# A transformer kernel with another order in its opening, and differential attention with the queries on the partitions

## The chip, the core and the metric

The kernel runs on one core of a Trainium2 chip. The metric is the device time of one execution in microseconds (us), lower is better. The engines have one instruction queue each and run what stands in it in that order: TensorE (PE in the profile; its weight loads are the row PEld), VectorE (DVE), ScalarE (ACT), GpSimd (POOL) and SyncE (SP, which only issues DMAs here; ACT issues some as well).

## The reference, cut to what matters

Two blocks for 512 tokens of width 1024, all float32. What the change touches:

```
# block 1, opening
mod = silu(c) @ w_ada + b_ada;  shift, scale, gate = split(mod, 3)
h = rms_norm(x, g_pre) * (1 + scale) + shift
proj = h @ w_in                      # forget gates, k and v of the window attention, ...
# block 2
mem_h = rms_norm(mem, mem_norm_g);   k, v = split(mem_h @ w_mem_kv, 2)   # 256 memory rows
k = rms_norm(k of 4 heads of 256)
# differential attention, 8 heads, two maps of depth 64 each, values 128 wide
p = softmax(q_m @ k_m.T * scale + bias, causal)       # m = 0, 1
a = p[0] - lam * p[1]
o = rms_norm(a @ v, subln_g) * (1 - lambda_init)
o = o * silu(gate);   y_diff = o @ w_proj
```

The rest (forgetting attention, window attention with sinks, convolution, cross attention to the memory, merging gates, projections) is computed by both kernels in the same way.

## The kernel before, in words

Every product of 1024-wide operands is made in three passes: an operand is split into a rounded part (`wh`, `hh`) and the rest (`wl`, `hl`), and hh·wh, hh·wl and hl·wh are summed in one PSUM bank. `load_w` fetches a weight chunk in four (512 columns) or two DMAs, ACT casts it to `wh` (L170), DVE or POOL subtracts to get `wl` (L172). `mm_T` (L202), `mm_N` (L213) and `mm_W` (L221) issue the matmuls. PSUM has eight banks: three `mm`, two `sc` (scores), two `tp` (transposes), one `pv`.

**Opening.** Everything in it is issued through `Ordered` (all its rows have L342), so that each engine keeps the written order. The memory rows `mt` are transposed to `mT`; `mem_k(0, ...)` makes the first half of the memory keys, 16 float32 matmuls of 512 columns, each of which the profile shows as two passes; `mem_k(1, ...)` makes the second half in four pieces that stand between the other work. x (`xn`) is squared, normalised and transposed (`x_transpose`) to `xt`. For each of the eight 128-wide slices k, 1 MB of `w_ada` (`ada`) is multiplied with silu(c): `products` does it on ACT and DVE with two matmuls at the end (`sums`), `sums_pe` does it wholly on PE, with 16 matmuls of one column. `modulate` and `hidden` then make `hh` and `hl` of that slice: ACT writes `hh`, DVE the exact value `ht`, POOL or DVE the difference. The first projection (`w1c`, 264 columns, 96 matmuls of L213) stands behind the opening, then `qb` (96 matmuls of 512 columns, L221). SP issues the DMAs of the opening in the written order. The scheduler of the language orders the rest by priorities and a model of its own.

**Middle.** Between the output projection of block 1 and block 2, `mem_v(0)` and `mem_v(1)` make the memory values, 48 matmuls each in three passes (`sc<-wh,mh` and so on, L221), while the two norms of the block end are computed.

**Differential attention.** `staged` runs over 32 pairs (head h, 128 queries n): `diff_sc` makes the scores of two maps and exponentials, `diff_tp` transposes the probabilities, `diff_pv` multiplies with the values. After each step `fill` issues a few matmuls of projections (`glu`, `dqk`, `dv`, gates) between them. DVE also does the convolution there, 248 instructions of 512 columns (`cv`, L1020) at the lowest priority. `diff_pv` works once per head, with values as weights: 12 matmuls of 512 to 128 columns give the output with the value index on the partitions. The norm over that index is then a sum over partitions: `rsum` (four one-column float32 matmuls), `rsqrt_small`, `rdiag` (four diagonal tiles on DVE, L260) and `rbc` (four float32 matmuls, L266).

Of the kernel before, what the change touches and what calls it, by code (L numbers as in the profile page):

```python
# [20 lines left out]
P = 128  # L21
# [71 lines left out]
def two_block_kernel(ctx: ExitStack, tc: tile.TileContext, A: dict, out: bass.AP):  # L93
# [137 lines left out]
    def rsqrt_small(wk, ss, n, inv, eps, tag, bufs=None):  # L231
# [4 lines left out]
        dve.tensor_scalar(out=v, in0=ss, scalar1=inv, scalar2=eps, op0=ALU.mult, op1=ALU.add)  # L236
# [106 lines left out]


    mT_d = dram.tile([P, KT, 256], F32, name="mT_d")
    mrs = const.tile([P, 2], F32, name="mrs")
    with ExitStack() as st:
# [3 lines left out]
        mt = pa.tile([P, 2, 1024], F32, tag="ada", name="mt", bufs=4)  # L351
# [3 lines left out]
        mk = pa0.tile([P, 2, 1024], F32, name="mk")  # L355
        kss = pa0.tile([P, 2, 4], F32, name="kss")
# [45 lines left out]
        pms = {}  # L402

        def sums(k):
            pms[k] = tp_tile()
            for j in range(2):
                pe.matmul(out=pms[k][:, j:j + 1], lhsT=accs[k][0][:, j * P:(j + 1) * P], rhs=ones[:, 0:1], start=True, stop=True)

        def sums_pe(k):
            pms[k] = tp_tile()  # L410
            for j in range(2):
                for i in range(KT):
                    pe.matmul(out=pms[k][:, j:j + 1], lhsT=adas[k][:, i, j * P:(j + 1) * P], rhs=cs[:, i:i + 1], start=(i == 0), stop=(i == KT - 1))

        def modulate(k):
            dve.scalar_tensor_tensor(out=mod[:, 2 * k:2 * k + 2], in0=pms[k][:, 0:2], scalar=0.5, in1=V("b_ada")[:, 2 * k:2 * k + 2], op0=ALU.mult, op1=ALU.add)
            dve.scalar_tensor_tensor(out=gs[:, k:k + 1], in0=mod[:, 2 * k + 1:2 * k + 2], scalar=1.0, in1=V("g_pre", k), op0=ALU.add, op1=ALU.mult)

        def hidden(k, eng):
            t = pa.tile([P, S], F32, tag="ht", name="ht", bufs=2)  # L420
            act.activation(out=hh[:, k, :], in_=xt[:, k, :], func=AF.Identity, scale=gs[:, k:k + 1], bias=mod[:, 2 * k:2 * k + 1])
            dve.tensor_scalar(out=t, in0=xt[:, k, :], scalar1=gs[:, k:k + 1], scalar2=mod[:, 2 * k:2 * k + 1], op0=ALU.mult, op1=ALU.add)
            eng.tensor_tensor(out=hl[:, k, :], in0=t, in1=f(hh[:, k, :]), op=ALU.subtract)

        kb_ = [None, None]

        def mem_k(c, ks_):
            if ks_[0] == 0:
                kb_[c] = [sc_tile() for t in range(2)]
            for k in ks_:  # L430
                for t in range(2):
                    pe.matmul(out=kb_[c][t], lhsT=mT[:, k, t * P:(t + 1) * P], rhs=raws[c][k // 2][:, k % 2, :], start=(k == 0), stop=(k == KT - 1))

        def mem_k_out(c):
            for t in range(2):
                act.activation(out=mk[:, t, c * NW:(c + 1) * NW], in_=kb_[c][t], func=AF.Copy, scale=mrs[:, t:t + 1])
# [22 lines left out]
        mem_k(0, range(KT))  # L459
# [3 lines left out]
        act.dma_start(out=mT_d, in_=mT)  # L463
        products(0, act)
        products(0, dve)
        products(1, act)
        products(1, dve)
        load_ada(4)
        dve.tensor_copy(out=mrs, in_=rsqrt_small(pa, mss, 2, 1.0 / 1024, 1e-6, "rn2"))
        squares(xn, xss, range(NT))  # L470
        mem_k_out(0)
        mem_k(1, range(2))
        sums(0)
        sums(1)
        r = rsqrt_small(pa, xss, NT, 1.0 / 1024, 1e-6, "rn4")
        for t in range(NT):
            dve.tensor_scalar(out=xn[:, t, :], in0=xn[:, t, :], scalar1=r[:, t:t + 1], scalar2=None, op0=ALU.mult)
        modulate(0)
        modulate(1)
        products(2, act)  # L480
        products(2, dve)
        load_ada(5)
        x_transpose(range(4))
        products(3, act)
        products(3, dve)
        raw_chunk(1, range(2, 4))
        load_ada(6)
        x_transpose(range(4, KT))
        mem_k(1, range(2, 4))
        sums(2)  # L490
        hidden(0, pool)
        hidden(1, pool)
        products(4, act)
        products(4, dve)
        load_ada(7)
        sums(3)
        modulate(2)
        sums_pe(5)
        hidden(2, pool)
        modulate(3)  # L500
        hidden(3, pool)
        sums(4)
        products(6, act)
        products(6, dve)
        modulate(4)
        hidden(4, pool)
        modulate(5)
        hidden(5, pool)
        mem_k(1, range(4, 7))
        sums(6)  # L510
        mem_k(1, range(7, 8))
        mem_k_out(1)
        sums_pe(7)
        modulate(6)
        hidden(6, dve)
        modulate(7)
        hidden(7, dve)
# [22 lines left out]
        with low(-ROTP):  # L540
# [4 lines left out]
            dve.tensor_scalar(out=sub8, in0=V("subln"), scalar1=0.8, scalar2=None, op0=ALU.mult)  # L545
# [7 lines left out]


        with low(LOWMK):
            for t in range(2):
                sq = xn[:, t, :]
                act.activation(out=sq, in_=mk[:, t, :], func=AF.Square)
                dve.tensor_reduce(out=kss[:, t, :], in_=sq.rearrange("p (h d) -> p h d", d=256), axis=AX.X, op=ALU.add)
            kr = rsqrt_small(pa0, kss.rearrange("p t h -> p (t h)"), 8, 1.0 / 256, 1e-6, "kr")  # L560
            for t in range(2):
                for h in range(4):
                    s = mk[:, t, h * 256:(h + 1) * 256]
                    dve.tensor_scalar(out=s, in0=s, scalar1=kr[:, t * 4 + h:t * 4 + h + 1], scalar2=None, op0=ALU.mult)
                nc.scalar.dma_start(out=k_d[:, t, :], in_=mk[:, t, :])
# [59 lines left out]
    with ExitStack() as stS:  # L625
# [18 lines left out]
        w = load_w(A["w1c"], 264)  # L644
        for t in range(NT):
            ps = mm_tile()
            mm_N(ps[:, 0:264], w, hh, hl, t, n=264)
            act.copy(out=natk[:, t, :], in_=ps[:, 0:256])
            dve.tensor_tensor(out=fz[:, t, :], in0=ps[:, 256:264], in1=V("fgate"), op=ALU.add)
# [256 lines left out]
    def mem_v(c, bank):  # L906
        if c == 0:
# [5 lines left out]
        mh, ml = MV[0]  # L913
        w = load_w(A["w_mem"][2 + c], NW)
        banks = [bank() for t in range(2)]
        yield from mm_W(banks, w, mh, ml, range(2))
        mv = mvp.tile([P, 2, NW], F32, tag="mv", name="mv")
        for t in range(2):
            act.activation(out=mv[:, t, :], in_=banks[t], func=AF.Copy, scale=mrs[:, t:t + 1])
        nc.scalar.dma_start(out=v_d[:, :, c * NW:(c + 1) * NW], in_=mv)  # L920
        yield

    with ExitStack() as st:
# [21 lines left out]
        for hf in range(2):  # L945
# [31 lines left out]
            run(mem_v(hf, sc_tile))  # L977
# [9 lines left out]
    with ExitStack() as st:  # L987
        wk = open_pool(st, "wk2", 2, reuse_waits="tile")
        dp = open_pool(st, "dp", 2, reuse_waits="tile")
        cm_[0] = open_pool(st, "cm2", 1, reuse_waits="tile")  # L990
# [152 lines left out]
        def diff_tp(it):  # L1143
            h, n = it
            causal_tp(it, D.pop(it), n, (n + 1) * P, ("dpt", h))
# [417 lines left out]
```

## Time and profile before

| | |
|---|---|
| median of 3 runs | 1201.15 us (1197.31 to 1202.04) |
| profiled execution: time, span from first to last instruction | 1197.03 us, 1195.2 us |
[...]
| busy share of the span: PE, DVE, ACT, POOL | 97%, 74%, 46%, 16% |
| bytes moved | 167.34 MB, 140 GB/s on the mean |

A busy PE is not a PE at its peak, since the ends of matmuls are modelled; what a stretch of matmuls takes is best read from the starts of its first and last one. "Idle before" names what ended a wait. [...]

### The profile page before, as it was taken

How to read it: one execution, taken by the hardware profiler on the slowest of the kernel's cores; microseconds unless marked ns; L12 is line 12 of the kernel's file. 1: busy time of each engine (PE TensorE's matmuls, PEld its weight loads, DVE VectorE, ACT ScalarE, POOL GpSimd, SP SyncE). 2: the span in 40 equal slices, each digit the busy share in tenths (PEclk: the TensorE clock that was granted, in tenths of full speed). 3: DMA queues.
4: the chain of work that ended last, by engine and by line, in shares of the span. 5: the costliest groups of instructions: out<-in, count | busy, mean ns of one | idle time of the engine just before them, and what ended most of it. 6: DMA issues, size and time to landing. Idle time of an engine off the chain costs nothing.

```text
span 1195.2 us, 16262 instructions
## 1 busy us (share of the span) xinstructions
PE 1157.5 (97%) x5656; PEld 949.9 (79%) x5656; DVE 883.1 (74%) x1910; ACT 548.6 (46%) x1154; POOL 192.7 (16%) x145
## 2 busy tenths in 40 slices
PE   6899999999899999999999999999999999999998
PEld 3677877767588888888887788888888888888887
DVE  4767686658578499999999999999793478454342
ACT  4445665537665454554443643355432245242231
POOL 0233000101122201112020121022011131111100
PEclk9789999999999999999999999999999999999999
DMA  9724222354387323433332443344346855422233
GB/s 366 301 83 147 81 80 82 110 157 122 115 274 236 94 85 105 115 107 104 92 105 88 142 134 113 102 134 136 124 143 201 316 167 201 143 94 96 92 106 106
DMA packets 59073, 167.34 MB, mean 140 GB/s; under 512 B 7056, under 2 KB 10384, under 8 KB 57712
## 3 DMA queue, kind: packets, MB, share of 16 engines
q1 hardware_dynamic: 35968, 123.45, 32.3%
q10 hardware_dynamic: 23024, 42.86, 10.2%
q8 instruction: 44, 0.72, 0.2%
q14 instruction: 37, 0.30, 0.1%
HBM read 137.85 MB, written 21.63 MB: 133 GB/s over the span
## 4 chain that ended last, share of the span: by engine, by line
PE 76%; DVE 17%; issue 2%; ACT 2%; DMA 2%; SPq 0%; ACTq 0%; DVEq 0%
PE mm L202 41%; PE mm L221 18%; DVE cv L1020 6%; PE mm L213 2%; PE sc L221 2%; PE sc L342 2%; DVE wl L172 1%; PE pv L870 1%; PE mm L806 1%; DMA xn<-in_xn_dram 1%; PE pv L1317 1%; PE tp L847 1%; PE tp L342 1%; DVE dp L1140 1%; PE sc L1274 1%
## 5 line engine op out<-in xcount | busy, mean ns | idle before, releaser
L170 ACT CAST wh<-raw 128x512 fp32r<-128x512 f32 (+1 forms) x360 | 214.0, 616 | 203.3 <-PE mm L202 111.9
L172 POOL TENSOR_TENSOR wl<-raw,wh 128x512 fp32r<-128x512 f32 (+1 forms) x90 | 126.8, 1409 | 856.4 <-ACT wh L170 803.4
L172 DVE TENSOR_TENSOR wl<-raw,wh 128x512 fp32r<-128x512 f32 (+1 forms) x270 | 192.0, 723 | 92.7 <-ACT wh L170 89.8
L202 PE MATMUL mm<-hh,wh 128*128 128x512 f32 x640 | 252.1, 394 | 0.0
L202 PE MATMUL mm<-hh,wl 128*128 128x512 f32 x640 | 251.1, 393 | 0.4 <-DVE wl L172 0.4
L202 PE MATMUL mm<-hl,wh 128*128 128x512 f32 x640 | 250.6, 392 | 0.0
L1020 DVE SCALAR_TENSOR_TENSOR cv<-u,vec,cv 128x512 f32<-128x512 f32 x240 | 192.7, 803 | 1.9
L202 PEld LDWEIGHTS mm<-hh,wl 128*128 128x128 f32 x640 | 120.2, 188 | 25.5 <-DVE wl L172 0.6
L202 PEld LDWEIGHTS mm<-hh,wh 128*128 128x128 f32 x640 | 120.3, 188 | 24.0 <-issue 0.5
L202 PEld LDWEIGHTS mm<-hl,wh 128*128 128x128 f32 x640 | 120.3, 188 | 23.8 <-issue 0.2
L221 PE MATMUL mm<-wh,hh 128*128 128x512 f32 x256 | 100.0, 395 | 1.3 <-ACT xqn L1060 1.3
L221 PE MATMUL mm<-wl,hh 128*128 128x512 f32 x256 | 100.8, 394 | 0.3 <-DVE wl L172 0.3
L221 PE MATMUL mm<-wh,hl 128*128 128x512 f32 x256 | 100.5, 395 | 0.0
L202 PE MATMUL mm<-bh,wh 128*128 128x512 f32 x192 | 75.2, 392 | 0.0
L202 PE MATMUL mm<-bh,wl 128*128 128x512 f32 x192 | 74.7, 389 | 0.0
L202 PE MATMUL mm<-bl,wh 128*128 128x512 f32 x192 | 74.7, 389 | 0.0
L1135 ACT ACTIVATE dp<-dp,dst 128x128 f32<-128x128 f32 (+3 forms) x64 | 35.9, 561 | 75.6 <-DVE dst L1133 75.5
L221 PEld LDWEIGHTS mm<-wh,hh 128*128 128x128 f32 x256 | 48.1, 188 | 11.0 <-ACT xqn L1060 1.8
L221 PEld LDWEIGHTS mm<-wl,hh 128*128 128x128 f32 x256 | 48.1, 188 | 10.1 <-DVE wl L172 0.9
L221 PEld LDWEIGHTS mm<-wh,hl 128*128 128x128 f32 x256 | 48.1, 188 | 9.3
L213 PE MATMUL mm<-wh,hh 128*128 128x256 f32 (+1 forms) x160 | 46.1, 292 | 0.0
L213 PE MATMUL mm<-wl,hh 128*128 128x256 f32 (+1 forms) x160 | 45.7, 288 | 0.0
(345 smaller groups left out, 2102.9 us busy)
## 6 DMA issues: line engine op xcount, KB each, us to landing
raw<-in_w_dram SPq DMA_DIRECT2D x88, 512.0 KB
raw<-in_w_out_dram SPq DMA_DIRECT2D x24, 512.0 KB
raw<-in_w2n_dram SPq DMA_DIRECT2D x24, 512.0 KB
ada<-in_w_ada_dram SPq DMA_DIRECT2D x8, 1024.0 KB
rawm<-in_w_mem_dram SPq DMA_DIRECT2D x8, 512.0 KB
raw<-in_w1n_dram SPq DMA_DIRECT2D x8, 512.0 KB
wg<-in_w_gate_dram SPq DMA_DIRECT2D x8, 512.0 KB
raw<-in_w_mem_dram SPq DMA_DIRECT2D x8, 512.0 KB
```

The costliest lines, as they stand in the source:

```text
L170: act.copy(out=wh, in_=raw[:, s])
L172: eng.tensor_tensor(out=wl, in0=raw[:, s], in1=f(wh), op=ALU.subtract)
L202: m = pe.matmul(out=ps, lhsT=a[:, c0:c0 + P], rhs=at(b, k), start=(n == 0 and i == 0), stop=(n == KT - 1 and i == 2))
L213: pe.matmul(out=ps, lhsT=at(a, k)[:, t * P:(t + 1) * P], rhs=b[:, 0:n], start=(start and m == 0 and i == 0), stop=(stop and m == len(order ...
L221: x = pe.matmul(out=ps, lhsT=at(a, k)[:, t * P:(t + 1) * P], rhs=b[:, 0:n], start=(m == 0 and i == 0), stop=(m == KT - 1 and i == 2))
L342: return lambda *a, **k: tc.keep_in_program_order(fn(*a, **k))
L806: m = pe.matmul(out=pm, lhsT=csb[:, 2 * q + k, :], rhs=a[:, k, :], start=(q + k == 0), stop=(2 * q + k == KT - 1))
L847: pe.transpose(out=tp[:, j * P:(j + 1) * P], in_=pt_[:, j * P:(j + 1) * P], identity=ident)
L870: pe.matmul(out=pv[0:64, j * P:], lhsT=l_, rhs=r_[:, j, j * P:], start=(j == 0 and i == 0), stop=(j == NT - 1 and i == 2))
L1020: dve.scalar_tensor_tensor(out=a, in0=u[:, j:j + S], scalar=dw[:, m * 31 + j:m * 31 + j + 1], in1=a, op0=ALU.mult, op1=ALU.add)
L1135: act.activation(out=p_[:, :w], in_=p_[:, :w], func=AF.Exp, scale=-1.0, bias=st_[:, 0, n, m:m + 1], accum_out=st_[:, 1, n, m:m + 1])
L1140: dve.scalar_tensor_tensor(out=pms[0][:, :w], in0=pms[0][:, :w], scalar=rr[:, n, 0:1], in1=pms[1][:, :w], op0=ALU.mult, op1=ALU.add)
```

## The change

Five things are changed.

1. The second half of the memory keys leaves the opening. It is made in the middle, in the way of the values: `mem_v` becomes `mem_p(i, ...)`, called with i = 1 and 2 in the first half of the block end and with i = 3 in the second, and `mem_k_norm` norms the keys of one half.
2. The opening has another order. x is fetched ahead of `w_ada`; slice 2 moves from `products` to `sums_pe`; two of the four scalings of x and five `ht` move from DVE to ACT; all sums share one PSUM bank `pm`; `mT` is written to DRAM by SP behind `w1c`.
3. `w1c` is loaded and multiplied inside the opening, with the slice k as the outer loop over four banks, in the order 0, 1, 2, 5, 3, 7, 4, 6. The last slices of `hidden` stand between its matmuls.
4. `diff_sc` no longer normalises: p0 - lam·(s0/s1)·p1 is formed, which is s0 times the old one (s0 and s1 are the sums of exponentials). The norm that follows takes the factor out: its epsilon is multiplied by s0 squared.
5. `diff_pv` works once per pair (h, n), with probabilities as weights: per block of 128 keys one matmul over `vh` and `vl` side by side (256 columns) and one of the low probability part over `vh` (128 columns). The queries are on the partitions, so ACT sums the squares, POOL multiplies with the reciprocal root (`diff_norm`), and four transposes turn the result (`diff_out`).

```diff
-        raw_chunk(0, range(4))
-        load_ada(0, 1)
+        for q in range(4):
+            raws.append(pa.tile([P, 2, NW], F32, tag="rawm", name="rawm", bufs=4))
+            sp.dma_start(out=raws[q], in_=A["w_mem"][0][:, 2 * q:2 * q + 2, :])
         for t in range(NT):
             sp.dma_start(out=xn[:, t, :], in_=A["xn"][t])
-        raw_chunk(1, range(2))
-        load_ada(2, 3)
+        load_ada(0, 1, 2, 3, 4)
...
+        x_transpose(range(KT))
         sums(0)
+        sums_pe(2)
+        load_ada(5, 6, 7)
         sums(1)
...
+        sums_pe(5)
         sums(3)
-        modulate(2)
-        sums_pe(5)
...
+        sums_pe(7)
         sums(4)
         products(6, act)
+        modulate(5)
+        hidden(5, act, pool)
+        modulate(3)
+        hidden(3, act, pool)
+        w = load_w(A["w1c"], 264, on_pool=(1, 3), queue=sp)
+        sp.dma_start(out=mT_d, in_=mT)
         products(6, dve)
+        modulate(7)
+        hidden(7, act, pool)
         modulate(4)
...
+        hidden(4, act, dve)
+        wb = [sc_tile(), sc_tile(), pv_tile(), mm_tile()]
+        order = (0, 1, 2, 5, 3, 7, 4, 6)
+        for n, k in enumerate(order):
+            if n == 4:
+                sums(6)
+                modulate(6)
+                hidden(6, dve, dve)
+            wh, wl = w[k]
+            for t in range(NT):
+                for i, (a, b) in enumerate(((hh, wh), (hh, wl), (hl, wh))):
+                    pe.matmul(out=wb[t][:, 0:264], lhsT=a[:, k, t * P:(t + 1) * P], rhs=b, start=(n == 0 and i == 0), stop=(n == KT - 1 and i == 2))
+        mem_k_norm(pa0, mk, 0)
...
-            run(mem_v(hf, sc_tile))
+            for i in ((1, 2), (3,))[hf]:
+                run(mem_p(i, sc_tile))
...
-            dve.reciprocal(out=rr[:, n, :], in_=st_[:, 1, n, :])
-            dve.tensor_tensor(out=rr[:, n, 1:2], in0=rr[:, n, 1:2], in1=nlam, op=ALU.mult)
-            dve.tensor_scalar(out=pms[1][:, :w], in0=pms[1][:, :w], scalar1=rr[:, n, 1:2], scalar2=None, op0=ALU.mult)
-            dve.scalar_tensor_tensor(out=pms[0][:, :w], in0=pms[0][:, :w], scalar=rr[:, n, 0:1], in1=pms[1][:, :w], op0=ALU.mult, op1=ALU.add)
+            dve.reciprocal(out=rr[:, n:n + 1], in_=st_[:, 1, n, 1:2])
+            dve.scalar_tensor_tensor(out=rr[:, n:n + 1], in0=rr[:, n:n + 1], scalar=nlam, in1=st_[:, 1, n, 0:1], op0=ALU.mult, op1=ALU.mult)
+            dve.scalar_tensor_tensor(out=pms[0][:, :w], in0=pms[1][:, :w], scalar=rr[:, n:n + 1], in1=pms[0][:, :w], op0=ALU.mult, op1=ALU.add)
...
+            for j in range(n + 1):
+                v = vv[:, j, h % 2]
+                pe.matmul(out=pv[:, 0:256], lhsT=pth[:, j, :], rhs=v.rearrange("p a d -> p (a d)"), start=(j == 0), stop=False)
+                pe.matmul(out=pv[:, 0:P], lhsT=ptl[:, j, :], rhs=v[:, 0, :], start=False, stop=(j == n))
+            act.copy(out=o[:, n, :], in_=pv[:, P:256])
+            dve.tensor_tensor(out=o[:, n, :], in0=pv[:, 0:P], in1=o[:, n, :], op=ALU.add)
+            q = wk.tile([P, P], F32, tag="doq", name="doq", bufs=2)
+            act.activation(out=q, in_=o[:, n, :], func=AF.Square, accum_out=ss[:, n:n + 1])
...
+            r = rsqrt_small(wk, ss, NT, 1.0 / 128, ev, "or")
+            pool.tensor_tensor(out=o, in0=o, in1=r.unsqueeze(2).to_broadcast([P, NT, P]), op=ALU.mult)
...
+            ps = transposed(o, 0)
```

On PE, the start of the program before, a row for each run of like instructions (`sc<-rawm,mT` is `mem_k`, `tp<-cst,acc` is `sums`, `mm<-cst,xn` is `x_transpose`):

```order
L342 MATMUL mm<-cst,mt 128x128 x16
L342 MATMUL sc<-rawm,mT 128x512 x20
L342 MATMUL tp<-cst,acc 128x1 x4
L342 MATMUL mm<-cst,xn 128x128 x32
L342 MATMUL sc<-rawm,mT 128x512 x4
L213 MATMUL mm<-wh,hh 128x264
```

On PE, the same place of the changed kernel (`tp<-cs,ada` is `sums_pe`; numbers of buffers are shown, since the rows would read alike without them):

```order
L345 MATMUL tp_155<-cst_79,acc_241 128x1 x2
L345 MATMUL tp_155<-cs_106,ada_149 128x1 x16
L345 MATMUL tp_155<-cst_79,acc_256 128x1 x2
L345 MATMUL tp_155<-cs_106,ada_333 128x1 x16
L345 MATMUL tp_155<-cst_79,acc_341 128x1 x2
L345 MATMUL tp_155<-cs_106,ada_337 128x1 x16
L345 MATMUL tp_155<-cst_79,acc_366 128x1 x2
L345 MATMUL sc_495<-wh_437,hh_83 128x264
```

Ahead of these rows stand 16 memory-key matmuls and all 32 transposes of x. So the other 16 matmuls of the keys are gone from the opening, 16 one-column matmuls are new, and no projection stands between the sums any more.

On ACT, the end of the opening of the changed kernel (L345 are the ordered instructions; `hh` and `ht` of slices 7, 4 and then 6; the 512-wide casts are of `qb`):

```order
L345 CAST wh<-raw 128x264 x8
L522 COPY cst<-mod 128x1
L345 ACTIVATE hh<-xt,mod,gs 128x512
L345 ACTIVATE ht<-xt,mod,gs 128x512
L523 DMA cst<-in_cst_dram 128x1792
L170 CAST wh<-raw 128x512 x6
L345 ACTIVATE kq,kss<-mk 128x256 x3
```

Between the six casts and the last row stands the `hh` of slice 6. Before, the casts of `qb` stood behind every `hh`.

On PE, the value product of the first queries of the changed kernel, in the differential attention (`dpth` and `dptl` are the transposed probabilities, `dvv` both value parts):

```order
L1159 MATMUL pv<-dvv,dpth 128x256
L1160 MATMUL pv<-dvv,dptl 128x128
```

Ten such pairs stand there per head, in four groups with other work between them, and every group uses the one `pv` bank. In the forgetting attention ahead of it the order of the instructions on PE is the same in both kernels, and so it is from the cross attention to the end.

## Rows read from the trace of the kernel before

**Rows 1.** Head of the profile page.

```profile
span 1195.2 us, 16262 instructions
```

**Rows 2.** Three stretches: busy us of each engine, granted clock, DMA share, GB/s.

```profile
36.70:43.00 6.30, 4.32 (x34) 3.47 (x35) 6.14 (x18) 6.30 (x17) 1.24 (x1) 1.00 1.01 413
52.10:59.10 7.00, 6.99 (x33) 7.00 (x34) 6.20 (x12) 2.43 (x4) 2.65 (x2) 0.50 0.15 57
440.00:800.00 360.00, 352.86 (x1906) 301.87 (x1906) 351.65 (x804) 174.72 (x384) 60.06 (x36) 1.00 0.34 107
```

**Rows 3.** Chain that ended last: start us, us, what.

```profile
8.63 11.21 DMA xn<-in_xn_dram
366.95 10.88 PE sc L221 x48
```

**Rows 4.** Timeline of PE in the opening: start us, us, instruction, xcount.

```profile
9.97 14.41 PE L342 MATMUL sc<-rawm,mT 128*128 128x512 f32 x32
52.11 6.96 PE L342 MATMUL tp<-cs,ada 128*128 128x1 f32 x32 [2.32 <-issue]
59.79 8.29 PE L342 MATMUL sc<-rawm,mT 128*128 128x512 f32 x12
70.92 3.63 PE L342 MATMUL tp<-cs,ada 128*128 128x1 f32 x32
84.72 0.62 PE L221 MATMUL mm<-wh,hh 128*128 128x512 f32 x2
```

**Rows 5.** Timeline of ACT and DVE in the opening.

```profile
22.21 1.04 ACT L342 ACTIVATE xt<-xn 128x1024 f32<-128x1024 f32 x1
23.99 2.46 DVE L342 SCALAR_TENSOR_TENSOR acc<-ada,cs,acc 128x256 f32<-128x256 f32 x6
28.87 0.16 DVE L342 TENSOR_SCALAR rv<-xss 128x4 f32<-128x4 f32 x1
30.86 2.74 DVE L342 TENSOR_SCALAR xn<-xn,ry 128x1024 f32<-128x1024 f32 x4
43.70 1.56 ACT L342 ACTIVATE hh<-xt,mod,gs 128x512 fp32r<-128x512 f32 x2
82.52 3.22 ACT L170 CAST wh<-raw 128x512 fp32r<-128x512 f32 x6
```

**Rows 6.** Timeline of PE in the differential attention.

```profile
489.34 0.95 PE L251 MATMUL tp<-cst,doq 128*128 128x1 f32 x8
557.89 0.39 PE L1164 MATMUL pv<-ptl,dvh 128*128 128x512 f32 x1
559.30 0.28 PE L1164 MATMUL pv<-ptl,dvh 128*128 128x128 f32 x1
559.42 0.28 PE L1164 MATMUL pv<-pth,dvl 128*128 128x128 f32 x1
559.53 0.63 PE L292 MATMUL tp<-cst,qkn 128*128 128x128 f32 x4
705.35 1.13 PE L266 MATMUL tp<-rdiag,cst 128*128 128x128 f32 x8
```

**Rows 7.** Groups of DVE, 440 to 800 us: busy us, mean ns, idle before.

```profile
L1139 DVE TENSOR_SCALAR dp<-dp,drr 128x256 f32<-128x256 f32 (+3 forms) x31 | 16.0, 517 | 0.1
L260 DVE TENSOR_SCALAR rdiag<-cst,ry 128x128 f32<-128x128 f32 x32 | 10.7, 398 | 0.0
L1178 DVE SCALAR_TENSOR_TENSOR do<-do,sub,tp 128x512 f32<-128x512 f32 x8 | 5.9, 738 | 0.0
L850 DVE TENSOR_TENSOR ptl<-tp,pth 128x128 fp32r<-128x128 f32 x8 | 2.2, 281 | 0.0
```

**Rows 8.** Timeline of DVE and POOL near 446 us.

```profile
445.57 0.74 DVE L1020 SCALAR_TENSOR_TENSOR cv<-u,vec,cv 128x512 f32<-128x512 f32 x1
446.88 1.30 POOL L172 TENSOR_TENSOR wl<-raw,wh 128x512 fp32r<-128x512 f32 x1 [20.23 <-ACT wh L170]
446.91 1.81 DVE L1020 SCALAR_TENSOR_TENSOR cv<-u,vec,cv 128x512 f32<-128x512 f32 x1
```

More of the change, by code (lines that the diff above doesn't have):

```diff
@@ L423, in hidden @@
             eng.tensor_tensor(out=hl[:, k, :], in0=t, in1=f(hh[:, k, :]), op=ALU.subtract)
[L425 to L436, printed above, removed]
@@ L458, in two_block_kernel @@
                     act.activation(out=mT[:, k + j, :], in_=pj, func=AF.Copy, scale=g)
-        mem_k(0, range(KT))
+        kb_ = [sc_tile() for t in range(2)]
+        for k in range(KT):
+            for t in range(2):
+                pe.matmul(out=kb_[t], lhsT=mT[:, k, t * P:(t + 1) * P], rhs=raws[k // 2][:, k % 2, :], start=(k == 0), stop=(k == KT - 1))
         mss = pa.tile([P, 2], F32, tag="mss", name="mss", bufs=1)
@@ L462, in two_block_kernel @@
         squares(mt, mss, range(2))
-        act.dma_start(out=mT_d, in_=mT)
+        dve.tensor_copy(out=mrs, in_=rsqrt_small(pa, mss, 2, 1.0 / 1024, 1e-6, "rn2"))
+        squares(xn, xss, range(NT))
+        r = rsqrt_small(pa, xss, NT, 1.0 / 1024, 1e-6, "rn4")
         products(0, act)
+        for t in range(2):
+            dve.tensor_scalar(out=xn[:, t, :], in0=xn[:, t, :], scalar1=r[:, t:t + 1], scalar2=None, op0=ALU.mult)
+            act.activation(out=xn[:, t + 2, :], in_=xn[:, t + 2, :], func=AF.Copy, scale=r[:, t + 2:t + 3])
         products(0, dve)
@@ L467, in two_block_kernel @@
         products(1, dve)
[L468 to L472, printed above, removed]
+        x_transpose(range(KT))
         sums(0)
+        sums_pe(2)
+        load_ada(5, 6, 7)
         sums(1)
-        r = rsqrt_small(pa, xss, NT, 1.0 / 1024, 1e-6, "rn4")
-        for t in range(NT):
-            dve.tensor_scalar(out=xn[:, t, :], in0=xn[:, t, :], scalar1=r[:, t:t + 1], scalar2=None, op0=ALU.mult)
+        products(3, act)
@@ L478, in two_block_kernel @@
         modulate(0)
+        hidden(0, dve, pool)
+        for t in range(2):
+            act.activation(out=mk[:, t, :], in_=kb_[t], func=AF.Copy, scale=mrs[:, t:t + 1])
+        products(3, dve)
         modulate(1)
[L480 to L490, printed above, removed]
@@ L904, in two_block_kernel, with mem_p @@
     MV = {}
-    def mem_v(c, bank):
-        if c == 0:
+    def mem_p(i, bank):
+        if not MV:
             mh, ml = (mvp.tile([P, KT, 256], F32R, name=n) for n in ("mh", "ml"))
@@ L1149, in diff_pv @@
             if n == 0 and h > 0:
[L1150 to L1152 removed]
+                diff_norm(h - 1)
             if n == 2 and h > 0:
                 diff_out(h - 1)
[L1155 to L1160 removed]
@@ L1161, in diff_pv @@
-            for j in range(NT):
-                a, b = vh[:, j, c0:c0 + P], vl[:, j, c0:c0 + P]
-                for i, (l_, r_) in enumerate(((a, pth), (a, ptl), (b, pth))):
-                    pe.matmul(out=pv[:, j * P:], lhsT=l_, rhs=r_[:, j, j * P:], start=(j == 0 and i == 0), stop=(j == NT - 1 and i == 2))
-            o = wk.tile([P, S], F32, tag="do", name="do", bufs=3)
-            q = wk.tile([P, S], F32, tag="doq", name="doq", bufs=1)
-            act.activation(out=q, in_=pv, func=AF.Square)
```

181 lines of the change are left out of this document (84 added, 97 removed).

## The prediction

> **What bounds the kernel now.** I read the page's head first [rows 1] and its engine table: PE is busy 97% of 1195.2 us, so what leaves PE's queue is gained and what leaves another engine is gained only where PE waits for it. Then the busy time by stretch [rows 2]. In the differential attention PE and DVE are both full: of 360 us PE is busy 352.86 and DVE 351.65. So PE loses at most 7.1 us to waits there, and work taken from DVE can give back no more than these. The opening is different. At 36.7 to 43.0 DMA is saturated (1.01 at 413 GB/s) while PE only transposes. At 52.1 to 59.1 PE is busy, but at a granted clock of 0.50, and it does one-column sums. So PE's busy share there hides slow and thinly used time. The first matmul of `qb`, which begins the steady part, starts at 84.72 [rows 4]; I call this T0 and work out the new one. Everything behind it is costed as a difference.
>
> **Opening, PE's path.** `mem_k(0)` ends at 9.97+14.41 = 24.4 [rows 4] and is unchanged. x landed at 8.63+11.21 = 19.84 [rows 3]. Two slices of `w_ada` no longer go ahead of it: 2×1.05 MB at 413 GB/s is 5.1 us, so x lands near 15. It then needs four squares of 1.04, 2.0 for the root (28.87 to 30.86, until the scalings begin) and 2.74 for four scalings, now half on ACT [rows 5]: ready at about 22, ahead of PE's 24.4. Then:
> - 32 transposes: 34 such rows filled 6.30 us [rows 2], so 5.9, to 30.3.
> - `sums_pe` of slices 2, 5, 7. The 32 rows of one took 3.63 at the full clock and 6.96 at half [rows 4]. These follow each other with little between, as at 52 us where the clock was 0.50, so I take one at full and two at half: 17.6. Four short sums of 4 rows each take 0.45 to 0.87, say 2.6 together. To 50.5.
> - `w1c`, 96 matmuls of 264 columns. 48 of 512 took 10.88 [rows 3], 0.227 each, so 264 columns are 0.117 at the full clock and twice that at half. I take some 20 of them slow, until the clock comes back, as the `mem_k(1)` piece behind the first `sums_pe` was slow too (12 passes in 8.29, 0.69 each, against 14.41/32 = 0.45 at the start [rows 4]): 20×0.234+76×0.117 = 13.6. To 64.1.
>
> **Opening, the path through ACT and DVE.** Slices 5 and 3 of `hidden` begin when `sums_pe(5)` is done, near 42 by the same steps; four ACT operations of 0.78 (1.56/2 [rows 5]) end at 45. Eight casts of `w1c` (3.22/6 scaled by 264/512, 0.28 each) take 2.2. ACT's part of product 6 is bounded by DVE's part of a whole slice-piece, 2.46 [rows 5]. At 50.5 come slices 7 and 4 (four times 0.78), to 53.6; then six casts of `qb`, 3.22 [rows 5], and only behind them `hh` of slice 6, which ends at 57.6. DVE's difference and the last 12 matmuls of `w1c` (1.4 to 2.8) end near 61. The casts of `qb` are a new wait in this queue: they need weights which SP issues behind `ada` 5 to 7 (these wait for the buffer that `sums_pe(2)` frees, near 36), `w1c` and the write of `mT`: 3.1+1.1+1.0+2.1 MB at 413 GB/s is 18 us, so they land near 54, about when ACT gets to them. Both paths come to 61 to 64; with some handovers I put T0 at 66, with 60 (no slow matmuls, no handover) to 74 (all of `w1c` at half clock, +9) as bounds. The term is **-18.7** (-24.7 to -10.7). Of it, 16 matmuls of `mem_k(1)` are the bulk: 32 passes, 12 of which took 8.29, so 14 to 22 us.
>
> **Middle.** 48 matmuls of 512 columns come in: one more block like the 10.88 of `mem_v` [rows 3]. Nothing else hides there, as PE is the full engine: **+10.9** (9.5 to 12). In three passes, at the full clock, the same keys cost half of what they cost in the opening.
>
> **Differential attention, PE.** Per head `rsum` (0.95) and `rbc` (1.13) go [rows 6]. Four transposes (0.63 [rows 6]) come in. The product itself before: 12 matmuls, the last 11 of which run from 557.89 to 559.53, with the first (0.23) 1.87 us. After: ten blocks of a 256-column and a 128-column matmul. Starts of 128-column ones lie 0.11 to 0.12 apart [rows 6], and half of 0.227 is 0.11 for 256 columns; so a pair costs 0.23 and ten 2.3. If 128 columns streamed at 0.057 the ten would cost 1.7. I take 2.3, the measured spacing. Eight heads: 8×(2.3-1.87-0.95-1.13+0.63) = **-8.2**. The listed durations overlap at their ends: if the removed pieces are worth only two thirds of their listing and the pair costs 0.24, the term is -3 to -5; if the pair streams, -13.
>
> **Differential attention, DVE and POOL.** L1139, L260 and L1178 go: 16.0+10.7+5.9 = 32.6 us [rows 7]. New are 32 additions from PSUM (L850 is the nearest: 0.281) and 8 small operations of about 0.16 [rows 5], 10.3: net -22.3. Against it stand eight multiplications on POOL. A `cv` took 1.81 beside a POOL subtraction and 0.74 just before it [rows 8], so each may cost DVE 1.07: 8.6 at most. [...] DVE thus has 14 to 22 us more room, but its room is not the time: `cv` has the lowest priority and fills it, and PE can regain only part of its 7.1 us. Not normalising (three large DVE operations become one) lies wholly in this room. I take **-2** for the waits (-6 if nearly all of them go, +8 if rival 3 below is a third true).
>
> **Sum.** -18.7+10.9-8.2-2.0 = -18.0 against the profiled 1197.03, so 1179.0. The profiled execution is 4.1 below the median of the runs; at the median's level that is **1183**.
>
> **Rivals.**
> 1. *The clock stays at half longer.* If the transposes already pull it down, all three `sums_pe` cost 6.96 and the transposes up to twice, T0 is 70 to 71 and the time 1187. For it: 0.50 in 52.1 to 59.1 with PE busy. Against it: 1.00 at 36.7 to 43.0, where PE does nothing but transpose [rows 2]. [...] Chance 0.14.
> 2. *The weights of `qb` come late.* If the landing slips from 54 to 65 (SP stands behind `ada` 7, which waits for a `sums_pe`, and the write of `mT`, which was on ACT's queue, is now ahead), ACT stands at the first cast, `hh` of slice 6 with it, and PE at the last slice of `w1c`: T0 74, time 1191. Chance 0.10.
> 3. *Slower: one `pv` bank.* 32 groups, each must wait until ACT has copied and DVE has added from the bank of the one before, and DVE's addition stands behind `cv` of 0.74. If each group holds PE, that is up to 24 us and the time is 1207; it is slower by 0.5% from about 0.75 us per group on. Against it: there are 360/32, about 11 us between groups, other work stands between, and score and transpose banks already wait for DVE in the same manner with 7.1 us idle in all. Chance 0.06.
> 4. *The differential part gives nothing.* The spacing of the new pairs is 0.33 and more (the 256-column matmul changes its weights every time), so the product is 3.3 to 3.5 us per head and its saving is gone: 1191. The four 128-column rows at 0.11 to 0.12 also change weights each and speak against it. Chance 0.08.
>
> **Chances.** The forecast has 0.62, the rivals 0.38. A difference of 0.5% (6 us) is about what a measurement of this kernel can tell from no change. Only rival 3 ends slower; rivals 2 and 4 end at -10, and two of the rivals together, or an opening at its bound of 74 with waits of +8, end within 0.5%. So faster 0.82, same 0.12, slower 0.06. The range goes from 1172 (T0 at 62, pairs that stream, -4 -5 and -2 of waits) to 1196 (an opening at 74 and half of the differential saving, +8 and +5).
>
> **What would show it.** In the changed profile: the first `qb` matmul starts at 60 to 74; the transposes of x stand directly behind `mem_k(0)`, with the clock still 1.00; the sums in some 20 us with the clock falling to 0.50 in them; `w1c` in 11 to 16 us; a third block of 48 in the middle of 10.9 us; no `rdiag` and `doq` sums on PE; pairs at 0.23; DVE's busy time in the differential part 14 to 22 us less, if `cv` doesn't stretch. The forecast is wrong if PE's idle time between 440 and 800 rises above 15 us (rival 3), if PE waits in `w1c` for ACT's `hh` (rival 2), or if the clock is 0.50 from 25 on (rival 1).

## The result, and the profile after

| | before | changed |
|---|---|---|
| median | 1199.08 us (5 runs, 1197.31 to 1202.04) | 1207.15 us (5 runs, 1206.02 to 1209.95) |
| ratio to before | | 1.007, 95% interval 1.0046 to 1.0095 |
| span of the profiled execution | 1195.2 us | 1204.6 us |
| its mean granted TensorE clock (1 is full speed) | 0.989 | 0.979 |

The change made the kernel slower, by 0.7%. The forecast was 1183 us, with 1172 to 1196 as the range.

Where the time went is read from the starts of three matmuls that both kernels have: the first of the memory blocks in the middle, the first score product of the differential attention, and the last one of all. In the timeline of PE, the kernel before (start us, us, what):

```profile
331.40 0.61 PE L221 MATMUL sc<-wh,mh 128*128 128x512 f32 x2
428.26 0.22 PE L1130 MATMUL sc<-k,qs 128*128 128x128 f32 x1
```

The same view of the changed kernel, with the first `qb` matmul ahead (T0 of the prediction, 84.72 in [rows 4]):

```profile
77.97 0.62 PE L221 MATMUL mm<-wh,hh 128*128 128x512 f32 x2
328.26 0.62 PE L221 MATMUL sc<-wh,mh 128*128 128x512 f32 x2
442.50 0.22 PE L1119 MATMUL sc<-k,qs 128*128 128x128 f32 x1
```

The last matmul starts at 1191.18 and at 1200.57. So the part up to the memory block became 3.1 us shorter (331.40 to 328.26), the part from there to the differential attention 17.4 longer (96.86 to 114.24), and the rest 4.9 shorter (762.92 to 758.07). Together that is +9.4. The sum of the prediction had -18.7, +10.9 and -10.2 in these places, -18.0.

T0 alone says less than it seems: it moved from 84.72 to 77.97, but in the changed kernel 22 of the 96 `w1c` matmuls run behind the first `qb` matmul, and before none did. So the start of the memory block is the fairer mark for the opening.

**The opening waits.** PE's timeline of the changed kernel around the sums (the short `sums` of four rows left out):

```profile
24.00 3.89 PE L345 MATMUL mm<-cst,xn 128*128 128x128 f32 x32
28.09 4.59 PE L345 MATMUL tp<-cs,ada 128*128 128x1 f32 x32
43.77 6.99 PE L345 MATMUL tp<-cs,ada 128*128 128x1 f32 x32 [10.24 <-DVE mod L345]
51.47 6.96 PE L345 MATMUL tp<-cs,ada 128*128 128x1 f32 x32
63.39 0.59 PE L345 MATMUL sc<-wh,hh 128*128 128x264 f32 x1 [4.10 <-ACT wh L345]
```

The transposes stand directly behind `mem_k(0)` and the first `sums_pe` comes at 28.09, better than I had worked out. Then PE stands for 10.24 us, and what ends the wait is `mod` on DVE. DVE's timeline says why `mod` was late (`acc` are the products of slices 3 and 4):

```profile
33.57 0.16 DVE L345 SCALAR_TENSOR_TENSOR mod<-tp,vec 128x2 f32<-128x2 f32 x1 [5.12 <-PE tp L345]
34.49 3.46 DVE L345 SCALAR_TENSOR_TENSOR acc<-ada,cs,acc 128x256 f32<-128x256 f32 x6
40.02 3.17 DVE L345 SCALAR_TENSOR_TENSOR acc<-ada,cs,acc 128x256 f32<-128x256 f32 x6 [0.76 <-ACT acc L345]
43.57 0.15 DVE L345 SCALAR_TENSOR_TENSOR mod<-tp,vec 128x2 f32<-128x2 f32 x1
59.33 0.16 DVE L345 SCALAR_TENSOR_TENSOR mod<-tp,vec 128x2 f32<-128x2 f32 x1 [14.76 <-PE tp L345]
```

All sums now share the bank `pm`. `sums_pe(5)` writes columns of it, and `modulate(2)`, written ahead of it, reads others. The matmul waits for that read at 43.57, and the read stands in DVE's queue behind two slices of products. DVE itself had come late to these: the row at 33.57 is `modulate(0)`, which needs only `sums(0)`, done near 28, and stood 5.12 us until `sums_pe(2)` and `sums(1)`, written ahead of it, had gone into the same bank. The other way round, `modulate(5)` needs only what PE had finished near 51, but it starts at 59.33: it waits for the last write to the bank that is written ahead of it, that of `sums(4)`. The `hh` of slice 5 and, behind it on ACT, the casts of `w1c` follow only then, and PE stands 4.10 us more. Busy times by stretch (columns as in [rows 2]) show that nothing fills these holes:

```profile
33.60:43.80 10.20, 0.03 (x1) 0.03 (x1) 9.12 (x22) 3.58 (x6) 2.84 (x2) 0.50 0.53 203
43.80:59.30 15.50, 15.49 (x72) 15.40 (x72) 0.66 (x2) 1.72 (x3) 1.26 (x1) 0.50 0.00 0
59.30:63.40 4.10, 0.01 (x1) 0.01 (x1) 0.58 (x5) 3.29 (x6) 1.55 (x2) 0.50 0.00 2
```

First DVE works and PE stands, then PE works and DVE stands, then neither. The DMA moves nothing from 43.8 on either, since SP stands for 29.9 us ahead of the fourth load of `w1c`, until DVE's `wl` frees a buffer; that load goes out at 65.30. The 10.24 us stand between a read and a write of neighbouring columns of one bank. Why these wait for each other is not shown; bank and tile are the same here, so no run shows either which of the two the dependency goes by.

**The middle waits too.** Waits of PE, 320 to 390 us (us in total, times, longest):

```profile
PE sc L221 <- ACT mv L905: 5.7, 1, 5.7
```

The second of the three memory blocks follows the first with nothing between. It needs the two `sc` banks of the first, which ACT copies out at 344.31, behind other work in its queue:

```profile
344.31 1.24 ACT L905 ACTIVATE mv<-sc,mrs 128x512 f32<-128x512 f32 x2
```

PE ended the first block near 339, and the second starts at 345.03. The wait also cost more than its 5.7 us: over the next 5 us the granted clock was 0.69, and the second block took 12.4 us, where the first and the third took 10.9. Busy times of that stretch:

```profile
345.03:350.00 4.97, 4.97 (x16) 3.98 (x16) 4.72 (x10) 2.97 (x10) 1.28 (x1) 0.69 0.98 362
```

**The differential attention is shorter on PE.** There are no `rdiag` and no one-column sums, and pairs follow as forecast (start us, us):

```profile
547.27 0.33 PE L1159 MATMUL pv<-dvv,dpth 128*128 128x256 f32 x1
547.44 0.22 PE L1160 MATMUL pv<-dvv,dptl 128*128 128x128 f32 x1
547.50 0.34 PE L1159 MATMUL pv<-dvv,dpth 128*128 128x256 f32 x1
```

From one 256-column start to the next it is 0.23. But the stretch is as full of waits as before; 454 to 814 us of the changed kernel, against the third row of [rows 2]:

```profile
454.00:814.00 360.00, 352.77 (x1897) 300.17 (x1896) 347.61 (x779) 183.98 (x470) 69.19 (x45) 1.00 0.36 110
```

PE is idle 7.2 us, as it was (7.1), and DVE is busy 347.61 against 351.65: only 4 us less, where 14 to 22 were expected.

### The profile page after: what moved, and what is told of

Same layout as the page of the kernel before. It is cut to its first block, busy times and chain, and to the rows that moved or that the text cites. A ratio compares the mean times of both kernels' runs of the same rounds, so it can differ in the third digit from the quotient of the medians.

```text
span 1204.6 us, 16398 instructions
## 1 busy us (share of the span) xinstructions
PE 1153.9 (96%) x5668; PEld 954.6 (79%) x5668; DVE 880.2 (73%) x1877; ACT 566.1 (47%) x1260; POOL 206.7 (17%) x157
## 4 chain that ended last, share of the span: by engine, by line
PE 72%; DVE 19%; DMA 3%; issue 3%; ACT 2%; POOL 1%; SPq 0%; ACTq 0%; DVEq 0%; POOLq 0%
PE mm L202 40%; PE mm L221 15%; DVE cv L1010 5%; DVE wl L172 3%; PE sc L221 2%; PE tp L345 2%; PE mm L213 1%; DVE dp L1122 1%; PE sc L345 1%; PE pv L856 1%; PE mm L792 1%; DMA raw<-in_w_mem_dram 1%; PE sc L1274 1%; PE pv L1317 1%; DVE acc L345 1%
## 5 line engine op out<-in xcount | busy, mean ns | idle before, releaser
L170 ACT CAST wh<-raw 128x512 fp32r<-128x512 f32 x360 | 217.6, 620 | 217.1 <-PE mm L202 114.6
L172 DVE TENSOR_TENSOR wl<-raw,wh 128x512 fp32r<-128x512 f32 x270 | 203.1, 764 | 101.2 <-ACT wh L170 98.8
L172 POOL TENSOR_TENSOR wl<-raw,wh 128x512 fp32r<-128x512 f32 x90 | 129.6, 1440 | 824.4 <-ACT wh L170 760.6
L202 PEld LDWEIGHTS mm<-bl,wh 128*128 128x128 f32 x192 | 36.1, 188 | 7.7 <-issue 0.2
L202 PEld LDWEIGHTS mm<-bh,wh 128*128 128x128 f32 x192 | 36.1, 188 | 7.7 <-issue 0.2
```

Source lines behind the costliest of these rows:

```text
L170: act.copy(out=wh, in_=raw[:, s])
L172: eng.tensor_tensor(out=wl, in0=raw[:, s], in1=f(wh), op=ALU.subtract)
L202: m = pe.matmul(out=ps, lhsT=a[:, c0:c0 + P], rhs=at(b, k), start=(n == 0 and i == 0), stop=(n == KT - 1 and i == 2))
```

## The experiments

Each was timed in 5 rounds beside the kernel before on the same chip; the ratio is to that. The rows come from several chips, on which the median of before was 1199.0 to 1201.8, so between rows the ratio is the fairer figure. The stages are those above: to the memory block, from there to the differential attention, and the rest, in the profiled execution.

| kernel | median us | ratio, 95% interval | stages us |
|---|---|---|---|
| before | | | 331.4, 96.9, 762.9 |
| changed | 1207.15 | 1.007 (1.0046 to 1.0095) | 328.3, 114.2, 758.1 |
| open_two | 1197.47 | 0.9978 (0.9961 to 0.9995) | 315.7, 116.1, 758.0 |
| open_three | 1193.21 | 0.9941 (0.9922 to 0.9961) | 312.3, 116.3, 756.9 |
| mid_banks | 1201.61 | 1.0014 (0.9997 to 1.0031) | 327.5, 110.7, 758.0 |
| diff_only | 1189.25 | 0.9922 (0.9891 to 0.9953) | 329.2, 96.9, 756.3 |
| both | 1186.14 | 0.9902 (0.9885 to 0.992) | 311.4, 110.5, 757.8 |
| both_norm_act | 1186.32 | 0.9895 (0.9876 to 0.9914) | 315.0, 109.1, 755.6 |
| keys_open | 1202.47 | 1.0029 (1.0015 to 1.0043) | 337.1, 103.6, 756.5 |
| unnorm_only | 1197.33 | 0.9988 (0.9972 to 1.0005) | 327.1, 99.0, 763.2 |
| diff_old | 1214.32 | 1.0131 (1.011 to 1.0151) | 329.4, 116.2, 764.3 |
| both_out_late | 1185.99 | 0.9888 (0.9869 to 0.9907) | 311.9, 110.3, 755.8 |
| both_wl_dve | 1181.41 | 0.9851 (0.9828 to 0.9873) | 314.3, 110.3, 748.6 |
| before_wl_dve | 1199.74 | 0.9986 (0.9965 to 1.0007) | 332.9, 99.1, 764.0 |

The first stage of one profile is uncertain by some us: the opening of before stands unchanged in diff_only, unnorm_only and before_wl_dve, and its first `qb` matmul starts at 84.72, 80.48, 80.45 and 87.17. The clock goes with it: from 24 us to that start the mean granted clock was 0.80, 0.88, 0.88 and 0.81. The openings with three banks, keys_open aside, start theirs between 64.11 and 65.72.

**open_two**: two banks for the sums.

```diff
-        pm = tp_tile()
+        pms = {}
+        pa_, pb_ = tp_tile(), tp_tile()
+        for k in (0, 2, 1):
+            pms[k] = pa_
+        for k in (5, 3, 7, 4, 6):
+            pms[k] = pb_
```

> The changed kernel with the sums of slices 0, 2, 1 in one PSUM bank and those of 5, 3, 7, 4, 6 in a second. Theory (shared bank): the 10.2 us for which PE stood before sums_pe(5), until DVE had done modulate(2) behind two slices of products, goes; what is left is bounded by when slice 5 of w_ada has landed, so the second pair of sums ends 8 to 10 us earlier, near 50, and the time falls by 8 to 10 us, to 1197 to 1199. Rival (late slices): slices 5 to 7 come late anyway, since the DMA is full until 39 us, and PE waits for them instead: under 4 us of gain, 1203 or more.

It fell by 9.7 us, as the shared bank says. PE's instructions stand in the same order in both kernels, so the bank is all that differs for PE. **open_three** has in addition:

```diff
+        pc_ = mm_tile()
+        pms.update({7: pc_, 4: pc_, 6: pa_})
         sums_pe(5)
```

> As the one before, and the sums of 7 and 4 in a third bank, so that modulate(5) and modulate(3) need only the sums of 5 and 3. Theory: also hidden(5) and hidden(3), and the casts of w1c behind them on ACT, start about 8 us earlier than sums(4) ends; the 4.1 us before w1c go and a part of the waits within it: 4 to 6 us below the one before, 1192 to 1195. Rival: w1c is held by PE's own sums, or by the third and fourth load of w1c that SP holds until casts free a buffer: no more than 2 us below the one before.

It fell by 4.3 more. PE's timeline of open_three, to be held against that of the changed kernel above:

```profile
28.19 4.25 PE L345 MATMUL tp<-cs,ada 128*128 128x1 f32 x32
33.73 6.99 PE L345 MATMUL tp<-cs,ada 128*128 128x1 f32 x32 [0.43 <-DMA ada<-in_w_ada_dram]
41.43 6.97 PE L345 MATMUL mm<-cs,ada 128*128 128x1 f32 x32
49.11 0.57 PE L345 MATMUL sc<-wh,hh 128*128 128x264 f32 x1
```

The 10.24 became 0.43, now a wait for the slice itself, and the 4.10 ahead of `w1c` is gone: `w1c` begins at 49.11 and not at 63.39. So late slices were not the cause.

**mid_banks**: other banks for the second memory block.

```diff
-                run(mem_p(i, sc_tile))
+                run(mem_p(i, tp_tile if i == 2 else sc_tile))
```

> The changed kernel with the bank pair tp instead of sc for the second of the three memory blocks in the middle, so that it need not wait until ACT has copied the first block out. Theory (bank): the 5.7 us wait and the slow clock behind it go, 6 to 7.5 us, time 1200 to 1201. Rival (weights): ACT's casts of that block's weights are late as well, since the loads land late; PE then waits for wh instead and at most 2 us are won, 1205 or more.

It gave 5.5 us, a little less than expected, and 3.5 of it in this stage of the profile. The wait for the bank is gone, and 1.2 us of waits for `wl` on DVE and 0.4 of others came in; about 50 of the 540 matmuls of the stage also stand elsewhere in PE's order. Of the stage's excess of 17.4 over before, 13.9 is left (110.7 less 96.9): 10.9 of work, 1.85 of idle time on PE (before had none here), and 1.1 that these runs don't explain.

**diff_only**: the kernel before with parts 4 and 5 alone. The constant of the norm's gain stays that of before while the new code expects half of it, so the differential output is twice too large here.

> The kernel before with the new differential attention alone (not normalised, queries on the partitions, value parts side by side); opening and middle as before. Theory: it gives what the stretch gave in the changed kernel, 4.9 us, so 1194 against 1199 of before: 9.7 us of PE work less 4.8 us of waits. Rival A (the waits come from the shifted start, not from the change): 8 to 10 us, 1189 to 1191. Rival B (no gain at all by itself): within 2 us of before.

The median is 9.8 us lower. In the profile the third stage gives 6.6 of it and the opening, whose instructions are those of before, 2.2, which goes with its higher clock (0.88 for 0.80); the rest is between executions. So Rival A comes closest by the median, but the same waits stand in the stretch as in the changed kernel (2.1 for `dp`, 1.9 for POOL's product, 1.5, 1.0), so they are not from a shifted start: they belong to the new order.

**diff_old**: the reverse, the changed kernel with the differential attention of before.

> The changed kernel with the differential attention of before: only the opening and the middle are new. If the stages add up, the opening's -4.6 and the middle's +18.3 are left alone, 14 us above before: 1212 to 1214 (the changed kernel plus the 4.9 to 6.7 us that the new stretch gave). If the new differential attention gave nothing in this surrounding: 1206 to 1208.

1214.3, just above the expected range: the opening and the middle alone make the kernel 1.3% slower, and the new differential attention takes 7.2 us off (1214.32 to 1207.15). The stages add up.

**both**: open_three and mid_banks together.

> The changed kernel with three banks for the sums of the opening and the tp banks for the second memory block in the middle. If the two are independent, their gains add: 1207 less 14 less 5.5, so 1187 to 1188. If what the opening gives back is met again by a wait in the middle, since ACT and the loads there then stand earlier against PE: 1191 or more.

1186.1, 21 us below the changed kernel and 1% below before, a little more than the sum of the two gains (14.0 and 5.5). Its first `qb` matmul:

```profile
64.11 0.39 PE L221 MATMUL mm<-wh,hh 128*128 128x512 f32 x1
```

**keys_open**: open_three with the second half of the keys back in the opening.

```diff
         sums(4)
+        kb1 = [sc_tile() for t in range(2)]
+        for k in range(KT):
+            for t in range(2):
+                pe.matmul(out=kb1[t], lhsT=mT[:, k, t * P:(t + 1) * P], rhs=raws[4 + k // 2][:, k % 2, :], start=(k == 0), stop=(k == KT - 1))
+        mk1 = pa0.tile([P, 2, NW], F32, name="mk1")
+        for t in range(2):
+            act.activation(out=mk1[:, t, :], in_=kb1[t], func=AF.Copy, scale=mrs[:, t:t + 1])
...
-            for i in ((1, 2), (3,))[hf]:
+            for i in ((2,), (3,))[hf]:
```

> The changed kernel with three banks for the sums, and the second half of the memory keys made in the opening again, as 16 float32 matmuls behind the sums of slice 4, its 2 MB of weights loaded behind w_ada; the middle then has two blocks of 48 and not three, and no wait for a bank. Against open_three at 1193: the middle gives 10.9 + 7.4 = 18 us back; the opening pays 32 passes, 14 us at the full clock and more at half, less what of ACT's and DVE's work for w1c is then hidden behind it. If moving the keys was worth what I put on it, 8 us (18.7 of the opening's term is mostly theirs, less 10.9), the time is 1197 or more, once the middle's wait is taken out (it alone is worth 5.5: 1193 - 5.5 + 8 = 1195.5). If the keys fill time in which PE waits in any case, 1186 to 1190.

1202.5. PE's timeline of it:

```profile
48.58 16.86 PE L345 MATMUL sc<-rawm,mT 128*128 128x512 f32 x32
70.12 0.59 PE L345 MATMUL sc<-wh,hh 128*128 128x264 f32 x1 [4.69 <-ACT wh L345]
```

The keys take 16.86 us there against 10.9 in the middle, in line with what I put on moving them. But the edit brought waits of its own. The copies of the keys stand on ACT ahead of `hidden(5)` and hold it, and PE stands 4.69. In the middle PE waits again, for a cast of weights on ACT, so that two blocks took 103.6 us there where before took 96.9:

```profile
PE mm L221 <- ACT wh L170: 3.3, 1, 3.3
```

So the size, 16 us above both, is not clean; without the two waits it would be about 8 (an estimate, 16.3 less 4.7 and 3.3). The stretch between T0 and the memory block is another 5.7 longer than in both (253.0 against 247.3), so even this is no clean price of moving the keys.

**unnorm_only**: before with part 4 alone.

```diff
-            dve.tensor_scalar(out=pms[1][:, :w], in0=pms[1][:, :w], scalar1=rr[:, n, 1:2], scalar2=None, op0=ALU.mult)
-            dve.scalar_tensor_tensor(out=pms[0][:, :w], in0=pms[0][:, :w], scalar=rr[:, n, 0:1], in1=pms[1][:, :w], op0=ALU.mult, op1=ALU.add)
+            dve.scalar_tensor_tensor(out=pms[0][:, :w], in0=pms[1][:, :w], scalar=rr[:, n, 0:1], in1=pms[0][:, :w], op0=ALU.mult, op1=ALU.add)
```

> The kernel before with part 4 alone, probabilities that are not normalised, and the old differential product. The epsilon of the norm is left as it was, so its weight against the sum of squares is not that of the reference. Theory (DVE's time is cover): DVE loses 16 us of scaling, but PE's idle time between 440 and 800 is 7.1 us in all; within 2 us of before, 1197 to 1200. Rival (DVE bounds the stretch as much as PE): 4 us or more below before, 1195 or less.

No difference that can be told (0.9972 to 1.0005). DVE was busy 7.5 us less in the third stage (585.38 for 592.87) and PE idle 7.77 for 7.14. Waits changed their place: that for `rdiag`, 1.3 us before, is now the longest.

```profile
PE tp L266 <- DVE rdiag L260: 6.7, 2, 3.5
```

So the time taken off DVE bought nothing here. That all of it was cover is not shown, since the scheduler placed the stage anew: at least 300 of its 3734 matmuls stand elsewhere in PE's order.

**both_norm_act** and **both_out_late**: ACT instead of POOL for the product with the root, and `diff_out` one group later.

```diff
-            pool.tensor_tensor(out=o, in0=o, in1=r.unsqueeze(2).to_broadcast([P, NT, P]), op=ALU.mult)
+            for t in range(NT):
+                act.activation(out=o[:, t, :], in_=o[:, t, :], func=AF.Copy, scale=r[:, t:t + 1])
```

```diff
-            if n == 2 and h > 0:
+            if n == 3 and h > 0:
                 diff_out(h - 1)
```

> As the one before, and the multiplication with the reciprocal root in the differential attention is done by ACT (four scalings per head) instead of POOL (one of 512 columns per head). Theory (POOL costs waits): the 1.9 us that PE waits for POOL's product and the 6 us by which DVE's subtractions of the stretch got longer come back in part, 1 to 3 us below the one before. Rival (chance of the order): other waits take their place and the time is within 1 us, or above if ACT's 32 more operations come in the way of its casts.

> The kernel with three banks in the opening and tp banks in the middle, and diff_out one step later (with the fourth group of queries and not the third), so that its transposes no longer meet POOL's product unfinished. Theory (each wait shown counts by itself): the 1.9 us of it go, 1184 to 1185 against 1186. Rival: the wait moves, since the transposed output and its writing are later too: 1186 or more.

Both shorten the third stage by 2 us in the profile, and neither changes the median against both (1186.32 and 1185.99 against 1186.14). The first only changes the name of a wait (1.9 for POOL's product, then 2.0 for ACT's). Part of the 2 us is the clock: in both it was 0.50 from 695.2 to 698.6, behind the wait for `dp`; open_three and diff_only, with PE's instructions of this stage in the same order and no such stretch, took 756.9 and 756.3 for it, and these two 755.6 and 755.8. Whether anything is won is left open.

**both_wl_dve**: no weight subtraction of block 2 on POOL.

```diff
-        return load_w(A["w2"][W2C.index((name, i))])
+        return load_w(A["w2"][W2C.index((name, i))], on_pool=())
```

(and so for `w2n`). The reason is in the profile of both, DVE, POOL and PE near 694 us:

```profile
693.33 1.22 DVE L1134 SCALAR_TENSOR_TENSOR drr<-drr,nlam,dst 128x1 f32<-128x1 f32 x1
694.59 0.48 DVE L1135 SCALAR_TENSOR_TENSOR dp<-dp,drr 128x256 f32<-128x256 f32 x1
699.49 0.22 DVE L1134 SCALAR_TENSOR_TENSOR drr<-drr,nlam,dst 128x1 f32<-128x1 f32 x1
```

```profile
693.27 1.26 POOL L172 TENSOR_TENSOR wl<-raw,wh 128x512 fp32r<-128x512 f32 x1 [2.30 <-issue]
```

```profile
695.22 0.66 PE L1145 MATMUL tp<-cst,dp 128*128 128x128 f32 x2 [2.04 <-DVE dp L1135]
```

A DVE operation on one column took 1.22 us, about as long as the POOL subtraction beside it, and 0.22 alone; PE waited 2.04 for what stood behind.

> The same base, and all subtractions for the weights of block 2 on DVE, none on POOL. Theory (POOL's instructions stretch DVE's beside them, and one of these delayed a one-column operation from 0.22 to 1.22 us on the path of a 2.0 us wait of PE): that wait goes, 1184 to 1185. Rival (DVE has no room): 30 more subtractions of 0.69, 21 us, in a stretch in which DVE is full make PE wait for wl: 1188 or more.

1181.4, 4.7 below both and 1.5% below before: the best version, and more than the one wait of 2.04 was worth. 420 to 780 us of both, then of both_wl_dve:

```profile
420.00:780.00 360.00, 352.88 (x1906) 300.41 (x1904) 347.38 (x783) 183.28 (x472) 65.31 (x44) 1.00 0.36 109
```

```profile
420.00:780.00 360.00, 358.47 (x1948) 307.22 (x1947) 349.92 (x819) 188.54 (x480) 31.93 (x19) 1.00 0.37 113
```

PE's idle time fell from 7.1 to 1.5 us. DVE got 36 more instructions in the stretch, about 25 subtractions' worth of POOL's 33 us among them, and is busy only 2.5 us longer. Its subtractions took 0.71 us on the mean for 0.78, and its `cv` 0.79 for 0.81; the one-column operation, though, took 0.27 on the mean for 0.28, so that one was hardly stretched less. And the edit did one thing more: the scheduler placed the stage anew, and at least 400 of its 3702 matmuls stand elsewhere in PE's order. Whether the waits went with POOL's subtractions or with the order is not separated. **before_wl_dve** makes the same edit to the kernel before.

> The kernel before, with all subtractions for the weights of block 2 on DVE and none on POOL. If POOL's stretching of DVE is the whole matter, it gives the same as in the version above, 4 to 5 us: 1194 to 1195. If DVE's room, which the new differential attention made, is needed for it, the 21 us of subtractions meet a DVE that is busy 351.65 of 360 us: within 2 us of before or slower, 1197 or more.

No difference (0.9965 to 1.0007). So the edit is not worth 4 to 5 us by itself. That it needs the room which the new differential attention makes on DVE fits this, but the order of the stage changed here too, so it is not shown.

## Why the prediction was wrong

**The step that failed: the sums "follow each other with little between".** I took PE's path and the path through ACT and DVE as two chains that meet only at the end, and put both at 61 to 64. They cross in the bank `pm`, three times: `modulate(0)` waits for `sums(1)` (5.12 us of DVE), `sums_pe(5)` waits for `modulate(2)` behind the products (10.24 us of PE), and `hidden(5)`, which I let begin "when `sums_pe(5)` is done, near 42", waits for `sums(4)` (14.76 us of DVE, ahead of `modulate(5)`). The front part of the document had said that all sums share one bank; no step asked what that orders. Two banks gave 9.7 us and a third 4.3, and the rest of the working then held: T0 64.1 to 65.7 for 66, with 12 matmuls of `w1c`, 1.5 us, still behind it. The three `sums_pe` cost 18.5 (17.6 forecast), the 32 transposes 3.9 for 5.9: the 6.30 us that I scaled for them held 2 us in which PE was idle (4.32 busy in [rows 2]). Of the 24 us between forecast and result, the banks of the opening and the middle together (both) give 21 back.

**The middle: work right, wait missed.** 48 matmuls cost 10.9. The earlier values had stood one block to each half, so the trace of before showed no wait for a bank; I read that as a property of the block and not of its being alone. The 5.7 us wait, which mid_banks takes away, is the case of two blocks in a row over the same two banks, with ACT's copy between. The sum had no term for it, nor for the 1.5 us by which the second block was slower behind it.

**The differential attention: work right, the rest of the wrong sign.** From start to start on PE, the product took 17.5 us over all heads (18.4 forecast) and 3.5 for the transposes, against 30.8 of removed pieces: -9.7 for -8.2. The stage gave only 4.9, so +4.8 stands where I took -2 for waits. Some of it is idle time: the 30.8 hold the 1.3 us for which PE waited for `rdiag`, and without them PE is still idle 7.23 us in the whole stage (7.14 before), now for `dp`, POOL's product and the bank `pv` among others. Part of it is the clock. The changed kernel had a granted clock of 0.50 from 716.8 to 720.2, behind the 2.1 us wait for `dp`; diff_only, keys_open and open_three, with the same order on PE and no such stretch in this stage, took 756.3 to 756.9 for it against 758.1. The other 2 us or so stand in steps that count as busy, and these runs don't locate them. both_wl_dve, with the same matmuls in another order, is 14.3 below before in this stage, so these losses can be had back; whether from POOL or by the order is open.

DVE's room was wrong too: 4 us and not 14 to 22. Between the two stretches shown, `wl` went from 54.7 to 59.9 us and the one-column `drr` from 4.7 to 9.9, beside 45 POOL instructions for 36. My bound of 8.6 for POOL looked at the eight new products and `cv`, which has the lowest priority, and left these out. The lower branch of the PE term, -3 to -5, was also added up wrongly: with the removed sums at two thirds and the pair at 0.24 it is 8×(2.4-1.87-1.39+0.63), -1.8; nothing hung on it.

**The rivals.** Slower had a chance of 0.06 and came by none of the four. Rival 3, the one `pv` bank, gave the right sign by the wrong bank: PE's wait for it was 1.0 us in all. I asked of one shared bank what stands between its users, and did not ask it of the other two that the change shares. Rival 1 did not hold for the transposes: 24 to 28 had a granted clock of 1.00, and 32 took 3.89. The clock was 0.50 from 33.6 to 63.4, but PE stood for 14.3 of these 30 us, and two sums at half the clock were in the forecast. Rival 2's late weights did occur, behind the bank: SP stood 29.9 us at `w1c`. Rival 4 fell with the spacing of 0.23.

## What to carry to other kernels

When results of several steps are put in one PSUM bank, ask whether it acts as one lock, as `pm` did here: a write of PE waited 10.24 us for a read of other columns written ahead of it, and two reads of DVE waited 5.12 and 14.76 us for such writes. Before costing a moved block, list the banks that it takes and who empties them, since a block that never waited alone may wait behind its like, as the second memory block did for 5.7 us. Work taken from an engine that is not the bound may buy nothing by itself (unnorm_only: 7.5 us less of DVE, ratio 0.9988). And where an edit makes the scheduler place a stage anew, a change of a few us (both_wl_dve) is not yet a proof of the reason for which the edit was made: compare the order of the instructions before naming a cause.

## What the runs showed of the hardware

A one-column operation of DVE took 1.22 us beside a POOL subtraction of 1.26, and 0.22 without (the rows at 693 and 699 us above); it ended at 694.55, the subtraction at 694.53. I had reckoned this with `cv` alone. It was not so for every short operation. Beside one POOL product (555.55 to 556.59 us of both) the reciprocal took 0.17 us, as it did at 699.29 with no POOL instruction beside it, and the operation behind it took 0.58 and ended at 556.61, with the product:

```profile
555.55 1.04 POOL L1182 TENSOR_TENSOR do<-do,ry 128x512 f32<-128x512 f32 x1 [5.57 <-DVE ry L248]
555.83 0.17 DVE L1133 RECIPROCAL drr<-dst 128x1 f32<-128x1 f32 x1 [0.36 <-ACT dp L1131]
556.03 0.58 DVE L1134 SCALAR_TENSOR_TENSOR drr<-drr,nlam,dst 128x1 f32<-128x1 f32 x1
```
